# One row of norm weights spread by TensorE, and a hand-written order of half-block steps for the first tiles of a hybrid decoder trunk

## The chip, the cores and the metric

The kernel runs on one core of a Trainium2 chip. The metric is device time in microseconds, the median of several executions. Engines are named as in the profile: PE (TensorE, matrix products), ACT (ScalarE), DVE (VectorE), POOL (GpSimd) and SP (SyncE, which issues most of the DMA transfers).

## The reference

One layer of a decoder trunk over 1024 positions of 1024 features, with 16 learned meta tokens put in front (1040 rows). The part that matters here is its beginning:

```
def rmsnorm(x, gain):
    y = xf * lax.rsqrt(jnp.mean(xf * xf, axis=-1, keepdims=True) + EPS)
    return (y * gain)

h = concatenate([meta, x])
u = rmsnorm(h, mix_norm_pre)
proj = u @ w_in                 # 1024 x 4608
q, f_logit, i_in, g_out, v_pool, gate_a, gate_b = split(proj, cuts)
a = hgrn2(q, f_logit, i_in, g_out, ...)       # chunked linear recurrence
p = multiscale_pool(v_pool, ...)
z = sigmoid(gate_a) * (a @ w_branch_hgrn) + sigmoid(gate_b) * (p @ w_branch_pool)
h = h + rmsnorm(z @ w_out, mix_norm_post)
u = rmsnorm(h, ffn_norm_pre)
h = h + rmsnorm((gelu(dwconv(u @ w_gate)) * (u @ w_up)) @ w_down, ffn_norm_post)
```

The first columns that the kernel computes are those of `i_in` (512 columns), the "v" products.

## The kernel before, in words

Every fp32 product is made as three products of a shorter fp32 type: an operand is split into a `hi` part (a cast on ACT) and a `lo` part (a subtraction on DVE), and hi·hi, hi·lo and lo·hi are added up in a PSUM bank (`mm3`, lines 186 to 190).

The kernel begins with the rows. A tile is 128 rows. `vtiles` (L463) is the order in which the nine tiles (one of them the 16 meta rows) are taken. For each tile, `norm_steps` (L412) squares the row on ACT with a running sum, takes the root, makes the reciprocal on DVE, and multiplies row, reciprocal and gain in two halves (`scalar_tensor_tensor`, L420). The gain is a 128 x 1024 tile, `g1`, filled by one DMA that reads the 1024 weights once for every partition (`gain_bc`, L143). `feature_steps` (L426) then transposes the normalised row on PE in two groups of four, copies each group out of PSUM as `uhi` (L434, ACT) and subtracts for `ulo` (L436, DVE). The weights of the v products arrive in four blocks `raws` (`load_wi`, L457: two blocks of 128 rows by 512 columns each, side by side in one tile of 1024); `split_wi` (L511) casts one block whole (L516) and subtracts it whole (L517). The first three blocks' hi and lo parts lie in the buffers `whi` and `wlo`, three of each, which the later weights use again. `v_mm` (L520) makes the three products of one 128-row slice `k`.

Before the first row is ready, `warm` (L505) keeps PE busy with products of a constant matrix and the identity that go to an unused bank. Then the steps of tiles 0 and 1 follow in an order written out by hand, inside `tc.manual_schedule(engines={E.Activation, E.DVE, E.PE})`: on these engines the instructions run in the order in which they are written. On the others, SP among them, a planner orders them by its own timeline, and may put a later load ahead of an earlier store. Outside such blocks the planner orders all engines; that is so for the later stage of the recurrence heads.

After tiles 0 and 1 the loop over `vtiles[2:]` (L1081) makes each tile's 24 products, its features two tiles ahead, its norm four tiles ahead, sums of features that later products need (`gate_steps`, spread by `SUMS_AT`), and `v_out` (L530), which copies the bank out and stores it. In its last pass it makes `gl`, a `Loader` for two blocks of "G" weights: two loads into the raw buffers `wraw` (three of them), two casts and two subtractions into `whi` and `wlo` (`wsplit`, L149). Behind the loop come the first loads of the gate products (`gates.load_first`, L263 at the issue), the two G products, and then the gate products themselves, which a class `Strassen` makes by seven products P1 to P7 instead of eight. Units 0 to 3 begin with P1 and P2; `start_pair(2)` (L349) loads the pair of raw blocks of unit 0 (`load_unit`, L275 at the issue), of which POOL makes four sums (L282 to L285) for P5, P6, P7 and P3. `put_gate` stores results (L888).

Of the kernel before, what the change touches and what calls it, by code (L numbers as in the profile page):

```python
# [12 lines left out]
ALU = mybir.AluOpType  # L13
# [49 lines left out]
          "osg.2 sub2.2 sub32.1 sub8.1 wBA2 wBA6 wBA7 wBB2 wF0 wF2 wF3 wPP2 wPV0 wPV1 wQ0 wQ1 lq4.3 kdsub.1 qsmul.1 "  # L63
          "lk32.0 e1q.3 e1q.1 lq2.1 wQ2 sub2.3 rsl.0 lk32.3 lq64.1 qsmul.2").split()
TRUNC = False

CH_ALL = [(0, 348), (348, 346), (694, 346)]
CH_Q = [(0, CW), (CW, CW), (2 * CW, CW)]
# [3 lines left out]
def trunk_kernel(ctx: ExitStack, tc: tile.TileContext, x, meta_tokens, mix_norm_pre,  # L72
# [29 lines left out]
    def slot(n, dtype=F32, name="s"):  # L102
        return stage["fm", "p"].tile([P, n], dtype, tag="fm", name=nm(name), padded_shape=[P, LP])
# [17 lines left out]
    def small(shape, name, tag, bufs=4):  # L121
        return sm.tile(shape, F32, tag=tag, name=nm(name), bufs=bufs)

    def rr(a):
        return a.bitcast(F32)
# [7 lines left out]
    eps_t = const.tile([P, 1], F32, name="eps_t")  # L133
    dve.memset(eps_t, EPS)
    act.activation(small([P, 1], "std", "ns"), eps_t, AF.Sqrt)
    ident = const.tile([P, P], F32, name="ident")
    make_identity(nc, ident)
    onesm = const.tile([P, P], F32, name="onesm")
    pool_e.memset(onesm, 1.0 / P)
    onesr = const.tile([P, P], F32R, name="onesr")  # L140
    pool_e.tensor_copy(onesr, onesm)

    def gain_bc(src, name):  # L143
        t = slot(D, name=name)
        nc.sync.dma_start(t, src[0].partition_broadcast(P))
        return t
# [21 lines left out]
    class Loader:  # L168
# [10 lines left out]
        def next(self):  # L179
            self.at += 1  # L180
            return self.got[self.at - 1]
# [230 lines left out]
    def norm_steps(row, rows, gbc):  # L412
        ssq = small([P, 1], "ssq", "nq")
        un = slot(D, name="un")
        act.activation(un[:rows], row[:rows], AF.Square, accum_out=ssq[:rows])
        rstd = row_rstd(ssq, rows, "n")
        yield un
        for j in range(2):
            n = slice(j * 512, (j + 1) * 512)
            dve.scalar_tensor_tensor(un[:rows, n], row[:rows, n], rstd[:rows], gbc[:rows, n], ALU.mult, ALU.mult)  # L420
            yield un
# [29 lines left out]
    def load_row(t0, rows):  # L451
        row = slot(D, name="row")
        src = meta_tokens[:, :] if t0 == 0 else x[0, t0 - NM : t0 - NM + rows, :]
        nc.sync.dma_start(row[:rows], src)
        return row

    def load_wi(j):  # L457
        raw = slot(1024, name="wiraw")
        nc.sync.dma_start(raw.rearrange("p (k c) -> p k c", k=2), wblock(WIN, 2 * j, 2, CI, 512))
        return raw  # L460


    vtiles = [row_tiles[i] for i in (1, 5, 2, 6, 3, 7, 0, 4, 8)]  # L463
    rows_in = [load_row(*vtiles[0])]
    g1 = gain_bc(mix_norm_pre, "g1")
    raws = [load_wi(0)]
    rows_in.append(load_row(*vtiles[1]))
    raws += [load_wi(j) for j in range(1, 4)]
    rows_in += [load_row(*rt) for rt in vtiles[2:]]

# [34 lines left out]
    def warm(n):  # L505
        for _ in range(n):
            pe.matmul(junk_bank[:, :P], onesm, ident, start=True, stop=True)

    wi = []

    def split_wi(raw):  # L511
        if len(wi) < 3:
            hi, lo = (wst.tile([P, 1024], F32R, tag=t, name=nm(t)) for t in ("whi", "wlo"))
        else:
            hi, lo = slot(1024, F32R, "wihi"), slot(1024, F32R, "wilo")
        act.copy(hi, raw)  # L516
        dve.tensor_tensor(lo, raw, rr(hi), ALU.subtract)  # L517
        wi.append((hi, lo))

    def v_mm(ps, t0, k):  # L520
        hi, lo = wi[k // 2]
# [521 lines left out]

    vb = [bank("pv") for _ in range(2)]
    E = mybir.EngineType
    with tc.manual_schedule(engines={E.Activation, E.DVE, E.PE}):
        warm(14)
        n0, n1 = (norm_steps(rows_in[i], P, g1) for i in range(2))
        next(n0)
        next(n0)  # L1050
        un0 = next(n0)
        f0 = feature_steps(un0, P, uhi, ulo, vtiles[0][0])
        split_wi(raws[0])
        next(f0)
        next(f0)
        next(f0)
        next(n1)
        next(f0)
        next(n1)
        un1 = next(n1)  # L1060
        v_mm(vb[0], vtiles[0][0], 0)
        v_mm(vb[0], vtiles[0][0], 1)
        split_wi(raws[1])
        f1 = feature_steps(un1, P, uhi, ulo, vtiles[1][0])
        next(f1)
        next(f1)
        split_wi(raws[2])
        next(f1)
        next(f1)
        split_wi(raws[3])  # L1070
        for i, j in ((0, 1), (1, 0), (0, 2), (1, 1), (0, 3), (1, 2), (1, 3)):
            for k in (2 * j, 2 * j + 1):
                v_mm(vb[i], vtiles[i][0], k)
        v_norm(2)
        v_norm(3)
        for i in range(2):
            v_feat(2 + i)
            v_norm(4 + i)
        for i in range(2):
            v_out(vb[i], vtiles[i][0])  # L1080
        for i in range(2, len(vtiles)):  # L1081
            ps = bank("pv")
            for k in range(KD):
                v_mm(ps, vtiles[i][0], k)
            if i < 5:
                v_feat(i + 2)
            if i == 5:
                v_feat(7)
                v_feat(8)
            v_norm(i + 4)  # L1090
            if i == 3:
                params()
            if i == 5:
                for q in ("t2", "t1", "t3", "t4"):
                    two_halves(gq, q)
                sums = [gate_steps(d) for d in ds]
            if i == len(vtiles) - 1:
                gl = Loader([job("G", h)[:2] + (P,) for h in range(EARLY_G)])
            for j in SUMS_AT.get(i, ()):
                next(sums[j], None)  # L1100
            v_out(ps, vtiles[i][0])
        gates.load_first(0)
        gates.load_first(1)
        gates.ahead(2)
        for h in range(EARLY_G):
            src, n_k, xs, chunks, post = job("G", h)
            r = proj(None, 0, n_k, xs, chunks, ws=gl.next(), name="pg", by_bank=2 * h)
            if h == EARLY_G - 1:
                post(r)
            for j in SUMS_AT.get(9 + 2 * h, ()):  # L1110
                next(sums[j], None)
            if h < EARLY_G - 1:
                post(r)
            if h == 0:
                dve.tensor_tensor(vmeta[:NM], vm_hl[:NM], vm_low[:NM], ALU.add)
                gates.load_first(2)
                gates.ahead(4)
            for j in SUMS_AT.get(10 + 2 * h, ()):
                next(sums[j], None)

        close_pool("ps")
        open_pool("pf", 4, PSUM)
        gates.load_first(3)
        for e in range(0, EARLY, 2):
            p = gates.start_pair(e)
            for f in [f[i] for i in range(2) for f in p]:
                f()
                for j in SUMS_AT.get(13, ()) if e == 0 else ():
                    next(sums[j], None)
# [671 lines left out]
```

## Time and profile before

| what | value |
|---|---|
| median of 3 runs | 1330.11 us (1330.09 to 1330.13) |
| the profiled execution | 1330.1 us |
| its span, first to last instruction | 1328.4 us |
| PE busy | 1317.1 us, 99% |
| DVE, ACT, POOL busy | 970.7, 566.8, 440.4 us |

The profile shows one execution. In a row of the timeline the first number is the start in microseconds from the start of the span, the second the length; then come engine, line, operation, what is written and read, the shape, and how many such instructions are merged in the row. The bracket says how long the engine was idle before it and what ended the wait. In a row of windows there stand the length of the stretch and then the busy time of PE, PE's weight loads, DVE, ACT and POOL, the granted clock, the DMA share and GB/s.

### The profile page before, as it was taken

The numbers are of one execution on the slowest core, as the hardware profiler recorded it, in microseconds if no ns is written. First come the engines' busy times: TensorE is split into PE (matmuls) and PEld (weight loads), VectorE is DVE, ScalarE is ACT, GpSimd is POOL, SyncE is SP. The second block draws the span as 40 slices with busy tenths as digits, with TensorE's granted clock in tenths as the row PEclk, the third lists the DMA queues.
The fourth block names the chain that finished last, engine by engine and source line by source line (L and its number), as shares of the span: only waits on it lengthen the run. The fifth ranks groups of instructions, "written<-read, shape, count | busy, mean of one in ns | idle before, by whom it ended". The sixth has DMA issues, their size and how long they took to land.

```text
span 1328.4 us, 19923 instructions
## 1 busy us (share of the span) xinstructions
PE 1317.1 (99%) x7713; PEld 1177.6 (89%) x7713; DVE 970.7 (73%) x1229; ACT 566.8 (43%) x946; POOL 440.4 (33%) x327
## 2 busy tenths in 40 slices
PE   8999999999999999999999999999999999999997
PEld 7799899999999999987898888888888888888886
DVE  6765545389968777766578999888988885455758
ACT  5553333365556575235564222322222233444443
POOL 2015421226525720061025555545555652000000
PEclk9999999999999999999999999999999999999999
DMA  7134332411011157987686776676766799666644
GB/s 272 41 110 157 124 109 99 125 50 48 19 51 35 35 170 268 350 280 257 219 300 234 183 211 188 198 205 171 178 161 142 175 246 310 215 224 223 222 174 159
DMA packets 139665, 230.38 MB, mean 173 GB/s; under 512 B 9000, under 2 KB 77196, under 8 KB 139570
## 3 DMA queue, kind: packets, MB, share of 16 engines
q1 hardware_dynamic: 127506, 204.71, 45.3%
q0 software_dynamic: 12064, 24.38, 10.8%
q8 instruction: 61, 1.00, 0.3%
q14 instruction: 34, 0.28, 0.1%
HBM read 165.56 MB, written 86.53 MB: 190 GB/s over the span
## 4 chain that ended last, share of the span: by engine, by line
PE 95%; DVE 4%; DMA 0%; ACT 0%; issue 0%; SPq 0%; DVEq 0%
PE P L311 15%; PE P L312 15%; PE P L314 15%; PE pd L188 5%; PE pd L190 5%; PE pd L189 5%; PE pm L188 2%; PE pm L189 2%; PE pm L190 2%; PE sl L695 1%; PE ppv L208 1%; PE pbb L208 1%; PE ppv L212 1%; PE pbb L209 1%; PE ppv L209 1%; PE pbb L212 1%
## 5 line engine op out<-in xcount | busy, mean ns | idle before, releaser
L312 PE MATMUL P<-v,whi 128*128 128x512 f32 (+2 forms) x408 | 140.7, 353 | 0.0
L311 PE MATMUL P<-v,whi 128*128 128x512 f32 (+2 forms) x408 | 140.7, 352 | 0.0
L314 PE MATMUL P<-v,wlo 128*128 128x512 f32 (+2 forms) x424 | 135.1, 349 | 0.0
L1535 DVE TENSOR_TENSOR rot<-wraw,rot 128x1024 fp32r<-128x1024 f32 x31 | 38.0, 1225 | 72.3 <-ACT rot L1534 72.2
L282 POOL TENSOR_TENSOR swa<-wraw,wraw 128x512 f32<-128x512 f32 x28 | 42.3, 1510 | 133.0 <-DMA wraw<-in_ffn_w_gate_dram 69.3
L311 PEld LDWEIGHTS P<-v,whi 128*128 128x128 f32 x408 | 76.7, 188 | 10.4
L312 PEld LDWEIGHTS P<-v,whi 128*128 128x128 f32 x408 | 76.6, 188 | 10.2
L314 PEld LDWEIGHTS P<-v,wlo 128*128 128x128 f32 x424 | 74.0, 188 | 10.8
L256 ACT CAST whi<-wraw 128x512 fp32r<-128x512 f32 x78 | 46.1, 618 | 87.6 <-PE P L312 64.2
L190 PE MATMUL pd<-rot 128*128 128x512 f32 x272 | 82.1, 389 | 0.0
L189 PE MATMUL pd<-rot 128*128 128x512 f32 x272 | 82.1, 389 | 0.0
L188 PE MATMUL pd<-rot 128*128 128x512 f32 x272 | 81.1, 389 | 0.1
L1534 ACT CAST rot<-wraw 128x1024 fp32r<-128x1024 f32 x31 | 32.7, 1055 | 90.8 <-PE pd L190 89.4
L256 ACT CAST whi<-swa 128x512 fp32r<-128x512 f32 x56 | 33.4, 618 | 81.9 <-PE P L312 76.2
L1463 DVE SCALAR_TENSOR_TENSOR y<-g,par,y 128x1024 f32<-128x1024 f32 x44 | 64.5, 1467 | 0.8
L257 DVE TENSOR_TENSOR wlo<-swb,whi 128x512 fp32r<-128x512 f32 x56 | 59.9, 1075 | 6.9 <-ACT whi L256 6.9
L257 DVE TENSOR_TENSOR wlo<-wraw,whi 128x512 fp32r<-128x512 f32 x74 | 62.3, 864 | 2.7 <-ACT whi L256 2.7
L256 ACT CAST whi<-swb 128x512 fp32r<-128x512 f32 x56 | 33.4, 618 | 68.6 <-PE P L312 64.2
L188 PEld LDWEIGHTS pd<-rot 128*128 128x128 f32 x272 | 51.0, 188 | 11.1 <-DVE p L1471 0.5
L189 PEld LDWEIGHTS pd<-rot 128*128 128x128 f32 x272 | 51.1, 188 | 10.6
L190 PEld LDWEIGHTS pd<-rot 128*128 128x128 f32 x272 | 51.0, 188 | 10.6
L311 PE MATMUL P<-t4h,whi 128*128 128x258 f32 (+1 forms) x196 | 57.0, 307 | 0.0
(421 smaller groups left out, 4133.0 us busy)
## 6 DMA issues: line engine op xcount, KB each, us to landing
wraw<-in_w_in_dram SPq DMA_DIRECT2D x36, 512.0 KB, 4.0
yt<-ysum SPq DMA_DIRECT2D x33, 512.0 KB, 4.5
wraw<-in_ffn_w_gate_dram SPq DMA_DIRECT2D x26, 512.0 KB, 7.3
wraw<-in_ffn_w_up_dram SPq DMA_DIRECT2D x22, 512.0 KB, 6.1
wsum<-in_ffn_w_down_dram SPq DMA_DIRECT2D x22, 512.0 KB, 9.0
wraw<-in_w_out_dram SPq DMA_DIRECT2D x18, 512.0 KB, 5.5
ysum<-ys SPq DMA_DIRECT2D x11, 768.0 KB, 7.7
sa<-sscr SPq DMA_DIRECT2D x16, 513.0 KB, 6.8
```

What stands on the lines that cost most here:

```text
L188: pe.matmul(ps, ahi, bhi, start=first, stop=False)
L189: pe.matmul(ps, ahi, blo, start=False, stop=False)
L190: pe.matmul(ps, alo, bhi, start=False, stop=last)
L256: act.copy(hi, src)
L257: (pool_e if 4 <= i < 2 * self.early else dve).tensor_tensor(lo, src, rr(hi), ALU.subtract)
L282: pool_e.tensor_tensor(s1, a21, a22, ALU.add)
L311: pe.matmul(d, whi[:, k, :], xh[:, c : c + w], start=(k == 0 and onto is None), stop=False, **go)
L312: pe.matmul(d, whi[:, k, :], xl[:, c : c + w], start=False, stop=False, **go)
L314: pe.matmul(x[:, o : o + w], wlo[:, k, :], xh[:, c : c + w], start=False, stop=(k == 3), **go)
L1463: dve.scalar_tensor_tensor(a, g[:, j : j + SEQ], cvw[:, j, m : m + 1], a, ALU.mult, ALU.add)
L1534: act.copy(hi, src)
L1535: dve.tensor_tensor(lo, src, rr(hi), ALU.subtract)
```

## The change

The gain row is loaded once, as 4 KB in one partition, by a DMA that POOL issues ahead of making the identity. PE multiplies it with a row of ones into two PSUM banks, after 8 warming calls and ahead of 3 more (before: 14 in one go). Tile 0's own norm, `first_norm`, reads the gain from these banks. The broadcast load `g1` stays for the other tiles, and is issued behind row 1. Row 0 is loaded in two halves, and its square is taken in two halves. `split_wi` becomes a generator of four steps of half a block; the steps of norms (n), weight splits (s), features (f) and single products (m: hi·hi, x: hi·lo, y: lo·hi; first digit the tile, second the slice k) follow the list `START`. SP joins the engines of the written order, and the G weights' loader is made at `i == 6` and not in the last pass (i = 8).

```diff
+WARM = (8, 3)
+START = ("n0 n0 n0 s0 s0 f0 s0 s0 f0 f0 f0 m00 m01 x00 x01 y00 y01 n1 s1 n1 n1 s1 s1 s1 f1 f1 m02 y02 f1 x02 f1 "
+         "m03 y03 x03 m10 x10 y10 m11 x11 y11 s2 s2 s2 s2 m04 x04 y04 m05 y05 x12 y12 m13 x13 y13 x05 s3 s3 m12 s3 "
+         "s3 m06 x06 y06 m07 x07 y07 m14 x14 y14 m15 x15 y15 m16 x16 y16 m17 x17 y17")
...
     act.activation(small([P, 1], "std", "ns"), eps_t, AF.Sqrt)
+    grow = slot(D, name="grow")
+    nc.gpsimd.dma_start(grow[:1], mix_norm_pre[:, :])
     ident = const.tile([P, P], F32, name="ident")
     make_identity(nc, ident)
     onesm = const.tile([P, P], F32, name="onesm")
     pool_e.memset(onesm, 1.0 / P)
+    ones = slot(P, name="ones")
+    pool_e.memset(ones[:1], 1.0)
...
-    rows_in = [load_row(*vtiles[0])]
-    g1 = gain_bc(mix_norm_pre, "g1")
+    rows_in = [slot(D, name="row")]
+    halves = [slice(j * 512, (j + 1) * 512) for j in range(2)]
+    for n in halves:
+        nc.sync.dma_start(rows_in[0][:, n], x[0, vtiles[0][0] - NM : vtiles[0][0] - NM + P, n])
     raws = [load_wi(0)]
     rows_in.append(load_row(*vtiles[1]))
+    g1 = gain_bc(mix_norm_pre, "g1")
     raws += [load_wi(j) for j in range(1, 4)]
...
-    def split_wi(raw):
-        if len(wi) < 3:
+    def split_wi(j):
+        if j < 3:
...
-        act.copy(hi, raw)
-        dve.tensor_tensor(lo, raw, rr(hi), ALU.subtract)
         wi.append((hi, lo))
+        for n in halves:
+            act.copy(hi[:, n], raws[j][:, n])
+            yield
+        for n in halves:
+            dve.tensor_tensor(lo[:, n], raws[j][:, n], rr(hi[:, n]), ALU.subtract)
+            yield
+
+    def gain_row():
+        for n in halves:
+            ps = bank("gb")
+            pe.matmul(ps, ones[:1], grow[:1, n], start=True, stop=True)
+            yield ps
+
+    def first_norm(row):
+        ssq, un = [small([P, 1], "ssq", "nq") for _ in halves], slot(D, name="un")
+        for n, s_ in zip(halves, ssq):
+            act.activation(un[:, n], row[:, n], AF.Square, accum_out=s_)
+            if s_ is ssq[0]:
+                dve.tensor_scalar(s_, s_, 1.0 / D, EPS, ALU.mult, ALU.add)
+        std, rstd = small([P, 1], "std", "ns"), small([P, 1], "rstd", "nr")
+        act.activation(std, ssq[1], AF.Sqrt, bias=ssq[0], scale=1.0 / D)
+        dve.reciprocal(rstd, std)
+        yield un
+        for n, g in zip(halves, gain):
+            dve.scalar_tensor_tensor(un[:, n], row[:, n], rstd, g, ALU.mult, ALU.mult)
+            yield un
+
+    def v_part(i, k, part):
+        (uh, ul), (hi, lo) = (uhi, ulo), wi[k // 2]
+        t, c = slice(vtiles[i][0], vtiles[i][0] + P), slice((k % 2) * 512, (k % 2) * 512 + 512)
+        a, b = {"m": (uh, hi), "x": (uh, lo), "y": (ul, hi)}[part]
+        done[i] += 1
+        pe.matmul(vb[i], a[:, k, t], b[:, c], start=done[i] == 1, stop=done[i] == 3 * KD)
...
-    with tc.manual_schedule(engines={E.Activation, E.DVE, E.PE}):
-        warm(14)
-        n0, n1 = (norm_steps(rows_in[i], P, g1) for i in range(2))
...
+    with tc.manual_schedule(engines={E.Activation, E.DVE, E.PE, E.SP}):
+        warm(WARM[0])
+        gain = list(gain_row())
+        warm(WARM[1])
+        done = [0, 0]
+        steps = dict(n0=first_norm(rows_in[0]), n1=norm_steps(rows_in[1], P, g1))
+        for token in START.split():
+            kind, i = token[0], token[1:]
+            if kind in "mxy":
+                v_part(int(i[0]), int(i[1]), kind)
+                continue
+            if token not in steps:
+                if kind == "f":
+                    steps[token] = feature_steps(uns[int(i)], P, uhi, ulo, vtiles[int(i)][0])
+                else:
+                    steps[token] = split_wi(int(i))
+            un = next(steps[token], None)
+            if kind == "n":
+                uns[int(i)] = un
         v_norm(2)
         v_norm(3)
...
-            if i == len(vtiles) - 1:
+            if i == 6:
                 gl = Loader([job("G", h)[:2] + (P,) for h in range(EARLY_G)])
```

More of the change, by code (lines that the diff above doesn't have):

```diff
@@ L1045, in trunk_kernel @@
     E = mybir.EngineType
-    with tc.manual_schedule(engines={E.Activation, E.DVE, E.PE}):
-        warm(14)
-        n0, n1 = (norm_steps(rows_in[i], P, g1) for i in range(2))
[L1049 to L1073, printed above, removed]
+    with tc.manual_schedule(engines={E.Activation, E.DVE, E.PE, E.SP}):
[17 more added lines that the diff above has]
+                uns[int(i)] = un
         v_norm(2)
```

## The prediction

> **What bounds the kernel now.** I read the page first: how much of the span TensorE (PE) works, and which engine the chain that ended last runs through.
>
> ```profile
> span 1328.4 us, 19923 instructions
> PE 1317.1 (99%) x7713; PEld 1177.6 (89%) x7713; DVE 970.7 (73%) x1229; ACT 566.8 (43%) x946; POOL 440.4 (33%) x327
> PE 95%; DVE 4%; DMA 0%; ACT 0%; issue 0%; SPq 0%; DVEq 0%
> ```
>
> PE is busy for all but 11.3 us of 1328.4, and the chain is PE's own queue for 95%. So time is saved only where PE idles or does work that counts for nothing. The windows view says where that is.
>
> ```profile
> 0.00:24.00 24.00, 20.15 (x92) 16.35 (x93) 13.21 (x21) 12.88 (x22) 8.55 (x36) 1.00 0.94 329
> 24.00:110.00 86.00, 86.00 (x536) 77.74 (x535) 57.26 (x117) 46.66 (x106) 11.07 (x9) 1.00 0.29 94
> 300.00:480.00 180.00, 179.43 (x1408) 175.88 (x1407) 148.08 (x160) 104.03 (x170) 95.58 (x47) 1.00 0.13 38
> ```
>
> The second number after the length is PE's busy time. The first 24 us hold 3.85 us of idle PE; the next 86 us hold none, so whatever brings the first two tiles' products to their end earlier moves everything behind them by as much. Now the timeline of those 24 us (start, length, engine, line, operation).
>
> ```profile
> 0.80 0.20 POOL masks.py:197 MEMSET ident<- 128x128 f32 x1 [0.29 <-POOLq L1787]
> 1.53 5.91 PE L507 MATMUL pj<-ident,onesm 128*128 128x128 f32 x28 [1.53 <-POOL ident masks.py:199]
> 4.20 1.06 ACT L415 ACTIVATE un<-row 128x1024 f32<-128x1024 f32 x1 [1.91 <-DMA row<-in_x_dram]
> 5.17 0.19 ACT L415 ACTIVATION_READ_ACCUMULATOR un<-row 128x1 f32 x1
> 5.38 0.29 ACT L407 ACTIVATE std<-ssq,eps_t 128x1 f32<-128x1 f32 x1
> 5.71 0.16 DVE L409 RECIPROCAL rstd<-std 128x1 f32<-128x1 f32 x1 [4.78 <-ACT std L407]
> 6.56 1.43 DVE L420 SCALAR_TENSOR_TENSOR un<-row,rstd,g 128x512 f32<-128x512 f32 x2 [0.69 <-DMA g<-in_mix_norm_pre_dram]
> 7.47 1.23 PE L431 MATMUL pt<-ident,un 128*128 128x128 f32 x8
> 7.94 1.05 ACT L516 CAST whi<-wiraw 128x1024 fp32r<-128x1024 f32 x1 [2.26 <-DMA wiraw<-in_w_in_dram]
> 8.89 1.07 ACT L434 CAST uhi<-pt 128x512 fp32r<-128x512 f32 x2
> 9.02 1.23 DVE L517 TENSOR_TENSOR wlo<-wiraw,whi 128x1024 fp32r<-128x1024 f32 x1 [1.03 <-ACT whi L516]
> 9.53 0.49 PE L188 MATMUL pv<-whi,uhi 128*128 128x512 f32 x1 [0.82 <-ACT uhi L434]
> 10.18 0.68 DVE L436 TENSOR_TENSOR ulo<-pt,uhi 128x512 fp32r<-128x512 f32 x1
> 12.92 1.23 PE L431 MATMUL pt<-ident,un 128*128 128x128 f32 x8 [0.82 <-DVE un L420]
> 14.63 0.50 PE L189 MATMUL pv<-wlo,uhi 128*128 128x512 f32 x1 [0.24 <-DVE wlo L517]
> 24.04 1.91 PE L431 MATMUL pt<-ident,un 128*128 128x128 f32 x16
> ```
>
> The row lands at 4.2, the reciprocal is done at 5.87, and the first half of the normalised row then waits for the broadcast gain until 6.56. PE fills that time with 28 instructions that count for nothing (14 calls, so a plain f32 product is two instructions). Tile 0's transposes start at 7.47. Up to 14.63 PE waits by turns for copies, casts and subtractions; from there 41 products run to 24.04, 0.23 us each, without a hole. Transposes to end: 16.57 us.
>
> **The clock.** The 28 instructions take 0.211 us each; the last four and later ones of the same size do not:
>
> ```profile
> 6.82 0.62 PE L507 MATMUL pj<-ident,onesm 128*128 128x128 f32 x4
> 439.14 1.79 PE sb L763 x16
> 603.36 0.57 POOL L1244 DMA_DIRECT2D wlos<-wlo  x1 [0.30 <-POOL wlo L1243]
> ```
>
> Sixteen in 1.79 us are 0.112 each. So PE runs at half rate until about 6.7, some 5.2 us after its first instruction, although the windows view gives a granted clock of 1.00 for the stretch. The third row is what one DMA issue costs POOL, 0.57 us.
>
> **Part by part: the start.** The new gain path: POOL issues the 4 KB load of the gain row before it makes the identity. That issue takes 0 (if POOL makes the identity first) to 0.57 us; I take 0.57, as it is written first, so PE's warming starts at 2.10 and not at 1.53. The load itself has about 4.7 us (0.8 to 5.5) before PE asks for it. Eight warming calls are 16 x 0.213 = 3.41, to 5.51. Then the gain is spread by two f32 products of 512 columns: four instructions, each four times a 128-column one, 0.85 us at half rate and 0.45 at full rate (no such row in the trace; the bounds are these two, from the L507 and L763 rows). With the clock changing at 6.7 as now: the first ends at 6.36, the second at 6.96, the others at 7.4 and 7.85. Three warming calls, 6 x 0.11, end at 8.5. PE takes its queue in order, so tile 0's transposes start at 8.5, a full microsecond later than now, although the row in halves makes the reciprocal no later (about 5.45: the second half's square is half of 1.06, then 0.19, 0.29, 0.16 as in the rows). The gain's DMA wait of 0.69 goes; PE's own spreading is what is late in its place. Bounds of this start: 7.8 where the clock changes as the gain products begin and the issue is short, 9.6 where it changes only as they end.
>
> What follows, with the rows' lengths (STT 0.72, cast and copy of 512 0.55, DVE 0.62 to 0.68): un halves at 7.9 and 8.75; transposes 8.5 and 8.95; copies of uhi at 9.15 to 10.25; the casts of the first weight block were done by 6.7, ahead of them, where now the copy stands behind a 1.05 us cast; DVE then makes the two wlo halves by 10.05 and the ulo halves by 11.3. ACT squares row 1 from 10.2, std ends 11.7; DVE: reciprocal 11.9, un halves 12.7 and 13.4, wlo of block 1 at 14.0 and 14.65, ulo 15.25. PE: six products between 9.75 and 11.5, transposes 12.8, two products, transposes 13.7, four products, and at 15.05 it is free for tile 1 with 12 products done and nothing late ahead of it. 36 products x 0.23 = 8.3: end at 23.3. From the transposes that is 14.8 us against 16.57: the half-block steps and the new order are worth 1.75, and the start gives 1.0 of it back. Net 24.04 - 23.3 = **0.7 us gained**; with the bounds of the start 7.8 and 9.6, from 1.4 gained to 0.4 lost. The later place of the gain's broadcast load (behind row 1) is hidden: the first four and a half transfers of 512 KB at the 329 GB/s of the 0:24 row are 7.2 us, so by about 9 it is in, and the first use is at 11.95.
>
> **Part by part: SP in written order.** SyncE (SP) is now in the hand-written order, so loads no longer slip ahead of stores.
>
> ```profile
> 19.02 1.38 SPq L151 DMA_DIRECT2D wraw<-in_w_in_dram  x2
> 62.82 1.06 ACT L154 CAST whi<-wraw 128x1024 fp32r<-128x1024 f32 x1 [0.77 <-PE pv L190]
> 65.90 0.38 SPq L263 DMA_DIRECT2D wraw<-in_w_in_dram  x1
> 97.61 0.37 SPq L275 DMA_DIRECT2D wraw<-in_w_in_dram  x1
> 102.33 0.34 SPq L888 DMA_DIRECT2D sscr<-sg  x1
> 101.25 1.29 POOL L282 TENSOR_TENSOR swa<-wraw,wraw 128x512 f32<-128x512 f32 x1
> 105.09 0.62 ACT L256 CAST whi<-swa 128x512 fp32r<-128x512 f32 x1 [2.79 <-POOL swa L283]
> 105.61 0.58 ACT L346 COPY p<-P 128x514 f32<-128x514 f32 x1
> 112.19 0.29 PE L311 MATMUL P<-t2h,whi 128*128 128x258 f32 x1
> wraw<-in_w_in_dram SPq DMA_DIRECT2D x36, 512.0 KB, 4.0
> ```
>
> The G weights' loads (L151), issued at 19.02 now, will stand behind the store of vtile 5 and be issued near 55. Their casts (L154) wait in any case for tile 8's products to free the buffers, at 62.82, so PE loses nothing. But moved to i == 6 the casts stand on ACT ahead of two v copies and of sums, and hold ACT and DVE for some 8 us; the products of tiles 7 and 8 need neither, and the sums are used only from 112 on. I cost that at 0.
>
> The one place where the order bites is unit 0's pair of weight loads (L275). Its second half is issued at 97.61 now; in written order both stand behind the store of 102.33, so they go out at 102.7 and 103.1 and land near 107.5 (4.0 us median). POOL's sums, 1.29 each, start then and not at 101.25: the third, which P6 needs, ends at 111.4; the cast to 112.0; the copy behind it on ACT (the 105.61 row), which frees the bank pair that P6 writes, at 112.6. P6 starts at 112.19 now. The 7 us that lie between the 105.09 cast and 112.19 are thus used up, and about **0.4 us are lost** (bounds: 0 if POOL makes P6's sum second, 1.5 if the load and store share the DMA engines and land a microsecond later).
>
> **The sum.** The profiled execution took 1330.1 us for a span of 1328.4 (1.7 us lie around it), the median of the runs is 1330.11, so no scaling. 1330.1 - 0.7 + 0.4 = **1329.8**. Its own range, from the bounds: 1328.7 to 1332.0. A difference of 0.2%, 2.66 us, is about what a measurement of this kernel can tell from no change.
>
> **Rivals.** (a) Clock released early. PE reaches full rate as the eight warming calls end, at 5.5: the gain products take 4 x 0.45, transposes start at 7.9, the end is 22.7; 1330.1 - 1.3 + 0.4 = 1329.2. Against it: now the change comes 5.2 us after PE's start. Beside it: the Trainium skill, "TensorE: Matmul & The Clock Gate", Part 1, says that a busy window of about 3.4 us releases the clock and that these windows run freely; the earliest case of that rule is this rival, and the 5.2 us of the trace also fit it, with a first window only half filled. 0.15.
>
> (b) Slower: the spreading keeps PE cold. The place is PE's queue between 5.5 and 8.9: the gain products use one row of the array, and if they do not count as activity, or the gain row lands late and PE idles, all 22 warming instructions and the four long ones run at half rate: 2.1 + 22 x 0.213 + 4 x 0.85 = 10.2 for the transposes, which then cost 8 x 0.10 more, and the first six products up to 6 x 0.2. End 25.0 + 0.8 + 1.2 = 27.0, 3.0 later than now, and with the 0.4: 1333.5. It decides from a transpose start of about 9.8 with the clock still low. For it: no row shows a one-row product. Against: the warming fills the time before it. 0.12.
>
> (c) Faster by more than 0.2%: transposes at 6.6 or before (un is possible from 6.2), which needs short gain products and a clock released at once, or less waiting in 300 to 480, where DVE is 148 of 180 us busy and the order isn't written by hand: a new start can reorder it. PE's idle there is only 0.57 us by the view, so little is to be had. 24.04 - (6.4 + 14.8) = 2.8: 1327.3. 0.14.
>
> (d) The same reordering with the other sign, or loads that come later than costed: a few microseconds of PE idle in that stretch, say 3: 1332.9. 0.06.
>
> **How the numbers follow.** Forecast 0.53 and (a) 0.15 lie within 0.2%: together 0.68, less 0.01 of tail. Faster 0.14; slower 0.12 + 0.06 and that tail, 0.19. The range reaches from 1327.5, leaving out most of (c), to 1332.9, leaving out half or more of (b).
>
> **What would show it.** Right: the gain products as four rows of 0.45 to 0.85 us between 5.5 and 8; transposes of tile 0 at about 8.5; steady products from about 15, transposes of tiles 2 and 3 at 23.3; L275 behind L888; POOL's first sum near 107.5 and P6 with its start just held. Wrong: transposes at 10 with products of 0.4 us pitch (b), transposes before 7 (c), or PE idle that is not now there between 300 and 480 (c, d).

## The result, and the profile after

The changed kernel took 1334.66 us (median of 8 runs, 1332.91 to 1337.83) against 1330.12 us before (8 runs, 1330.07 to 1331.08): a ratio of 1.0033, 95% interval 1.0024 to 1.0042. It is slower by 0.33%, and outside the predicted range. The eight times lie in two groups, 1332.91 to 1333.30 (four runs) and 1336.02 to 1336.34 (three), with the profiled run, 1337.83, above both. The median is thus only the middle of the gap between the groups (between 1333.30 and 1336.02): no run took it. The later group lies well above the range, the early one just above its end of 1332.9. Why there are two groups 3.1 us apart is part of what has to be explained.

Page of the changed kernel: span, busy time by engine, the chain that ended last.

```profile
span 1336.1 us, 19929 instructions
PE 1321.0 (99%) x7711; PEld 1179.1 (88%) x7711; DVE 972.6 (73%) x1234; ACT 567.5 (42%) x952; POOL 441.7 (33%) x329
PE 93%; DVE 4%; DMA 2%; ACT 1%; issue 0%; POOL 0%; SPq 0%; DVEq 0%; ACTq 0%; POOLq 0%
```

PE is busy 3.9 us longer than before with two instructions fewer, so its instructions became longer, and its idle time grew by 3.8 us (15.1 against 11.3). The windows view says where (length, PE, PE's weight loads, DVE, ACT, POOL, granted clock, DMA share, GB/s).

```profile
0.00:24.00 24.00, 19.84 (x76) 15.07 (x77) 12.36 (x24) 13.84 (x28) 8.33 (x38) 1.00 0.80 289
110.00:300.00 190.00, 187.57 (x1225) 175.50 (x1224) 103.42 (x132) 76.54 (x125) 61.09 (x42) 1.00 0.36 114
300.00:480.00 180.00, 179.45 (x1416) 176.24 (x1415) 149.10 (x160) 104.08 (x172) 97.07 (x47) 1.00 0.13 38
```

In the first 24 us PE executes 76 instructions in place of 92, in about the same busy time. Between 110 and 300 it idles 2.43 us. Between 300 and 480 it idles 0.55 us, as before (0.57). Now the timeline of the start.

```profile
1.35 0.68 POOL L141 DMA_DIRECT2D grow<-in_mix_norm_pre_dram  x1 [0.84 <-POOLq L1820]
2.02 0.24 POOL masks.py:197 MEMSET ident<- 128x128 f32 x1
2.89 3.78 PE L518 MATMUL pj<-ident,onesm 128*128 128x128 f32 x16 [2.89 <-POOL ident masks.py:199]
4.87 0.63 ACT L544 ACTIVATE un<-row 128x512 f32<-128x512 f32 x1 [0.61 <-DMA row<-in_x_dram]
5.95 0.16 DVE L549 RECIPROCAL rstd<-std 128x1 f32<-128x1 f32 x1 [1.51 <-ACT std L548]
6.61 3.78 PE L538 MATMUL gb<-grow,ones 1*128 1x512 f32 x4
8.71 0.75 DVE L552 SCALAR_TENSOR_TENSOR un<-row,rstd,gb 128x512 f32<-128x512 f32 x1 [2.60 <-PE gb L538]
10.31 1.65 PE L518 MATMUL pj<-ident,onesm 128*128 128x128 f32 x6
11.75 1.92 PE L439 MATMUL pt<-ident,un 128*128 128x128 f32 x8
13.49 1.10 PE L560 MATMUL pv<-whi,uhi 128*128 128x512 f32 x2
16.80 0.63 PE L439 MATMUL pt<-ident,un 128*128 128x128 f32 x4 [1.27 <-ACT whi L529]
27.27 1.91 PE L439 MATMUL pt<-ident,un 128*128 128x128 f32 x16
```

POOL's issue of the gain row starts only at 1.35 and takes 0.68, and the identity stands behind it, so PE's first instruction is at 2.89, not at 1.53. The four gain instructions run from 6.61 to 10.31, 0.93 us each. The six warming instructions behind them, 1.44 us from start to start of what follows, and the eight transposes of tile 0 at 11.75, 1.92 us against 1.23 before, are at half rate as well. No engine makes PE wait between 2.89 and the products: it is slow, not idle. Tiles 2 and 3 start their transposes at 27.27 (before: 24.04), 3.23 us late.

Later on, at unit 0 of the gate products and at the passage from the gates to the heads:

```profile
105.54 0.34 SPq L930 DMA_DIRECT2D sscr<-sg  x1
105.98 1.55 SPq L283 DMA_DIRECT2D wraw<-in_w_in_dram  x3
112.14 1.29 POOL L290 TENSOR_TENSOR swa<-wraw,wraw 128x512 f32<-128x512 f32 x1 [7.61 <-DMA wraw<-in_w_in_dram]
114.64 1.28 POOL L291 TENSOR_TENSOR swa<-swa,wraw 128x512 f32<-128x512 f32 x1
115.96 0.62 ACT L264 CAST whi<-swa 128x512 fp32r<-128x512 f32 x1 [10.44 <-POOL swa L291]
116.48 0.58 ACT L354 COPY p<-P 128x514 f32<-128x514 f32 x1
117.12 0.39 PE L319 MATMUL P<-t2h,whi 128*128 128x258 f32 x1 [1.54 <-ACT p L354]
252.21 0.40 PE L216 MATMUL pf<-uhi,whi 128*128 128x348 f32 x1 [0.87 <-DVE sg L926]
565.87 0.42 PE L216 MATMUL pba<-ah,whi 128*128 128x342 f32 x1 [1.14 <-ACT whi L172]
```

The chain can be read downwards: store, the loads of unit 0 behind it, POOL's sum when they land, the third sum, ACT's cast of it, ACT's copy of the bank behind the cast, and P6 at 117.12. Before, P6 started at 112.19 without a wait. With the 3.23 us already lost it would start at 115.42; it starts 1.70 later, and 2.1 with the short waits inside it. At the passage (before: 245.88) 1.0 us more is lost, at the projection at 565.87 (before: 558.16) another 1.4. So the profiled run lost 3.2 + 2.1 + 1.0 + 1.4 = 7.7 us, and that is what the spans differ by (1336.1 against 1328.4). In the last 1.4 PE waits for a cast on ACT; the profile puts that wait down to a store (`kept9h`) that landed 7.7 us behind its issue, against 6.5 before. Without them this run would lie beside the later group, so by the times they come in some runs only.

### The profile page after: what moved, and what is told of

It reads as the page before. It is cut to its first block, busy times and chain, and to the rows that moved or that the text cites. A ratio compares the mean times of both kernels' runs of the same rounds, so it can differ in the third digit from the quotient of the medians.

```text
span 1336.1 us, 19929 instructions
## 1 busy us (share of the span) xinstructions
PE 1321.0 (99%) x7711; PEld 1179.1 (88%) x7711; DVE 972.6 (73%) x1234; ACT 567.5 (42%) x952; POOL 441.7 (33%) x329
## 4 chain that ended last, share of the span: by engine, by line
PE 93%; DVE 4%; DMA 2%; ACT 1%; issue 0%; POOL 0%; SPq 0%; DVEq 0%; ACTq 0%; POOLq 0%
PE P L319 14%; PE P L322 14%; PE P L320 14%; PE pd L196 5%; PE pd L197 5%; PE pd L198 5%; PE pm L196 2%; PE pm L197 2%; PE pm L198 2%; PE sl L737 1%; PE ppv L216 1%; PE pbb L216 1%; PE ppv L220 1%; PE pbb L217 1%; PE pbb L220 1%; PE ppv L217 1%
## 5 line engine op out<-in xcount | busy, mean ns | idle before, releaser
L320 PEld LDWEIGHTS P<-v,whi 128*128 128x128 f32 x408 | 76.6, 188 | 10.2
L319 PE MATMUL P<-t2h,whi 128*128 128x258 f32 (+1 forms) x196 | 56.9, 307 | 1.5 <-ACT p L354 1.5
```

The source lines that it names most:

```text
L319: pe.matmul(d, whi[:, k, :], xh[:, c : c + w], start=(k == 0 and onto is None), stop=False, **go)
L320: pe.matmul(d, whi[:, k, :], xl[:, c : c + w], start=False, stop=False, **go)
```

## The experiments

Each kernel ran 8 to 12 times beside the kernel before, which took 1330.13 to 1330.24 on these chips. Short names: "the spread" is the gain row's load by POOL, the products with ones and the split warming; "SP written" is SP in the written order with the G loader at `i == 6`. My first theory had two parts: the spread costs the start (late warming, then a clock not released), and SP written costs unit 0's weights.

**The changed kernel without SP written.**

```diff
-    with tc.manual_schedule(engines={E.Activation, E.DVE, E.PE, E.SP}):
+    with tc.manual_schedule(engines={E.Activation, E.DVE, E.PE}):
-            if i == 6:
+            if i == len(vtiles) - 1:
```

> The changed kernel with SP left to the planner and the G loader back in the last pass; spreading and half-block steps stay. Theory: no wait at P6 and none at the passage to the heads; what is left is the start, which differs between executions by the moment of the clock's release: some near 1330.1, some near 1333.3. Rival (these waits come from the late start and not from SP's order): still about 2.9 us more, 1333 to 1336.

1331.33 us (six runs from 1330.13 to 1331.33, five from 1333.21 to 1333.35), ratio 1.0009, 1.0001 to 1.0018. Timeline and windows of its profiled run, one of the early group (1330.13):

```profile
2.88 3.67 PE L518 MATMUL pj<-ident,onesm 128*128 128x128 f32 x16 [2.88 <-POOL ident masks.py:199]
6.47 1.98 PE L538 MATMUL gb<-grow,ones 1*128 1x512 f32 x4
9.16 1.37 PE L439 MATMUL pt<-ident,un 128*128 128x128 f32 x8
9.00:10.00 1.00, 1.00 (x10) 1.00 (x10) 1.00 (x3) 0.21 (x1) 0.97 (x3) 0.86 1.02 291
10.00:11.00 1.00, 1.00 (x4) 0.63 (x3) 1.00 (x2) 0.81 (x2) 0.00 (x0) 0.50 0.97 356
110.00:300.00 190.00, 190.00 (x1249) 178.52 (x1248) 106.29 (x135) 78.36 (x129) 57.80 (x39) 1.00 0.33 106
```

PE starts as late as in the changed kernel, but here the gain instructions take 1.91 us together and not 3.70, and the transposes start at 9.16. That is the difference between the two groups. The end of the two tiles is 0.09 us later than before. The idle time between 110 and 300 is gone.

The two rows of 1 us show something more. PE is busy all the time, and still the granted clock falls: 0.86 on average from 9 to 10, then 0.50; finer stretches put the fall at 9.7 and the return at 13.1. Of the 3.4 us ahead of the fall, 1.9 were the one-row gain products. So the clock was released by the warming, and lost again without any idle time. The loss costs little here, since PE has to wait for ACT behind it anyway (0.35 us at 13.66; with the clock high, in the run with 128 rows below, 1.26 at the same place).

**The kernel before with SP written, and nothing else.**

```diff
-    with tc.manual_schedule(engines={E.Activation, E.DVE, E.PE}):
+    with tc.manual_schedule(engines={E.Activation, E.DVE, E.PE, E.SP}):
-            if i == len(vtiles) - 1:
+            if i == 6:
```

> The kernel before with SP in the written order and the G loader at i == 6, and nothing else. Theory: a start as before (transposes of tiles 2 and 3 at 24.04), P6 of unit 0 held for 1.5 to 2 us behind the late load of its weights, 1.0 us at the passage to the heads: 1333.0, executions alike. Rival (the wait at the heads comes from the late start): 1332.0. Rival (SP's order costs nothing by itself): 1330.1.

1334.22 us (1332.91 to 1336.76), ratio 1.0028, 1.0019 to 1.0037. Its profiled run took 1333.05. Windows and timeline:

```profile
110.00:300.00 190.00, 187.85 (x1226) 175.78 (x1225) 105.57 (x135) 77.78 (x128) 60.79 (x41) 1.00 0.34 109
113.58 0.39 PE L311 MATMUL P<-t2h,whi 128*128 128x258 f32 x1 [1.26 <-ACT p L346]
248.68 0.40 PE L208 MATMUL pf<-uhi,whi 128*128 128x348 f32 x1 [0.88 <-DVE sg L884]
```

The two losses appear without the new start: P6 1.8 us late by its end, the heads 2.8 in all. The expected 1333.0 came in four of eleven runs; the executions are not alike, and what the runs above 1333.3 add, 1.2 us in the median, was not traced.

**The changed kernel with unit 0's loads ahead of the last store.** In the loop that makes and stores P1 and P2 of the early units, the loads go out before the last store.

```diff
-            for f in [f[i] for i in range(2) for f in p]:
+            for n_, f in enumerate([f[i] for i in range(2) for f in p]):
                 f()
+                if e == 0 and n_ == 2:
+                    gates.load_unit(gates.run[0])
```

> The changed kernel with the pair of loads for unit 0 written one product earlier, between the stores of the first two gate results. Theory: they land about 3 us earlier, P6 of unit 0 does not wait (offset against before stays level there, 1.9 us less), while the step of 1.0 us at the passage to the heads stays or goes with the choice of banks: time 1.9 to 2.9 us under the changed kernel in executions with the same start, 1330.1 to 1331.1 and 1333.2 to 1334.2. Rival (P6's wait has another cause, the casts or the banks): no step less than 1.5 us at P6, times as the changed kernel's.

1333.21 us: four runs from 1330.03 to 1330.20, one at 1331.91, five from 1333.21 to 1333.74, one at 1336.80; ratio 1.0016, 1.0006 to 1.0025. The start of its profiled run (1333.27) is that of the changed kernel, transposes at 11.75. But:

```profile
110.00:300.00 190.00, 190.00 (x1250) 178.52 (x1248) 106.87 (x135) 77.76 (x128) 60.84 (x42) 1.00 0.35 110
109.58 1.29 POOL L290 TENSOR_TENSOR swa<-wraw,wraw 128x512 f32<-128x512 f32 x1 [5.05 <-DMA wraw<-in_w_in_dram]
```

POOL's first sum starts 2.6 us earlier, P6 starts on time, and the 1.0 us at the heads go with it, although nothing was changed there. So one late pair of loads costs about 3 us, at two places (2.8 in the run before this one, 3.1 in the changed kernel). The two groups remain, at 1330.1 and 1333.3: they are made at the start.

**A gain product that fills all rows of the array.** The product has the same length, but is made of a constant 128 x 512 tile and `onesm`; tile 0's gain is left out.

```diff
+    full = slot(512, name="full")
+    dve.memset(full, 1.0)
...
-            pe.matmul(ps, ones[:1], grow[:1, n], start=True, stop=True)
+            pe.matmul(ps, onesm, full, start=True, stop=True)
```

> The changed kernel, but the two gain products read a full 128-row constant instead of one row (tile 0 is left without its gain). Same number, width and place of PE instructions. Theory (a one-row product holds PE but does not count as the activity that releases its clock): now the clock is released during or before the second gain product in every execution, transposes at 8.7 to 10, and the slow group of executions near 1336 goes: all near 1333, median 1333.0. Rival (only the moment at which the clock is looked at decides): still two groups 3 us apart, 1333 and 1336, median near 1334.7.

1332.75 us, ten runs in one group from 1332.23 to 1333.81 and one at 1338.30; ratio 1.0023, 1.0014 to 1.0032.

```profile
6.45 1.98 PE L540 MATMUL gb<-full,onesm 128*128 128x512 f32 x4
8.94 1.04 PE L441 MATMUL pt<-ident,un 128*128 128x128 f32 x8
0.00:24.00 24.00, 19.63 (x94) 15.97 (x95) 14.29 (x27) 13.85 (x28) 8.76 (x38) 1.00 0.80 290
```

With one row in use, the later group held four of eight runs in the changed kernel, and five and six of eleven without SP written and with the early loads; with 128 rows, at most one of eleven. The profiled run has the clock released ahead of the gain products, like the one without SP written (gain products from 6.45 here, from 6.47 there); but with 128 rows the granted clock stays at 1.00 to the end of the start. The start ends 0.4 us earlier than before, and the loss that is left is SP's.

**Warming split 6 and 5.** The kernel with the early unit 0 loads, the same work on PE, but less of it ahead of the one-row products.

```diff
-WARM = (8, 3)
+WARM = (6, 5)
```

> The kernel with unit 0's loads ahead of the store, and the eleven warming calls split 6 and 5 in place of 8 and 3; nothing else. The work on PE is the same, and without a hole, from 2.89 on: 12 warming instructions of 0.23 to 5.7, the four gain instructions, 10 warming instructions. Theory (one-row products don't count towards releasing the clock): what stands ahead of the gain products is now 2.8 us of counted work in place of 3.7, too little to release it in any execution, so all are as the later group was with 8 and 3: gain products 0.9 each, transposes of tile 0 at 11.8, 1333.2 to 1333.8, and none near 1330.1. Rival 1 (one-row products count, and the two groups come from something else at the start): the unbroken work is the same, so the two groups stay, 1330.1 and 1333.3, in shares like 5 and 6 of 11. Rival 2 (what matters is only how long PE has worked, by any product): one group near 1330.1 to 1330.5, transposes at 9.2.

1333.37 us, eleven runs from 1333.21 to 1335.30 and one at 1329.69; ratio 1.0022, 1.0014 to 1.0031.

```profile
2.88 2.93 PE L518 MATMUL pj<-ident,onesm 128*128 128x128 f32 x12 [2.88 <-POOL ident masks.py:199]
5.74 3.78 PE L538 MATMUL gb<-grow,ones 1*128 1x512 f32 x4
11.74 1.91 PE L439 MATMUL pt<-ident,un 128*128 128x128 f32 x8
```

Theory: none early; it was one of twelve. The two rivals wanted half or all of them early. In the profiled run PE works without a hole from 2.88 on and is still at half rate past 11.74; by their times, so are eleven of the twelve. What it works on from 5.74 to 9.45 has one row. The share of early runs thus goes by the work ahead of the one-row products, not by all unbroken work.

**The gain row loaded by SP, behind the row's halves.**

```diff
-    nc.gpsimd.dma_start(grow[:1], mix_norm_pre[:, :])
...
+    nc.sync.dma_start(grow[:1], mix_norm_pre[:, :])
     raws = [load_wi(0)]
```

> The changed kernel with the 4 KB gain row loaded by SP behind row 0's halves, so that POOL makes the identity first. Theory (1.36 us of the late start are POOL's DMA issue): PE's warming starts at 1.5 and not at 2.9, the whole start moves 1.4 us earlier in executions with the same clock, but still two groups: 1332 and 1335. Rival (POOL's issue is hidden): no change against the changed kernel.

1334.71 us: three runs from 1331.62 to 1332.08, five from 1334.66 to 1335.08, one at 1336.76; ratio 1.0027, 1.0018 to 1.0037. In its profiled run (1331.65) the gain products start at 5.37 and the transposes at 8.05, and the two tiles end 1.3 us earlier than before; the SP losses are unchanged. Here the granted clock stays at 1.00 behind the one-row products: they do not make it fall in every run. POOL's issue thus costs the start 1.2 to 1.4 us, and has nothing to do with the two groups.

**The row in halves, alone.** The kernel before, with row 0 loaded by two transfers.

```diff
-    rows_in = [load_row(*vtiles[0])]
+    rows_in = [slot(D, name="row")]
+    for j in range(2):
+        nc.sync.dma_start(rows_in[0][:, j * 512 : (j + 1) * 512], x[...])
```

> The kernel before with row 0's load cut into two halves and nothing else. Theory (two loads of 2 KB pieces at the head of the queue slow what stands behind them): the broadcast gain lands at 8.4 to 8.9 and not at 6.5, the transposes start 1.5 to 2.3 us later, 1331.6 to 1332.5. Rival (the late gain of e1 and e3 came from something else): within 0.3 us of the kernel before.

1333.05 us (1332.17 to 1335.72), ratio 1.0023, 1.0014 to 1.0032.

```profile
8.78 1.41 DVE L420 SCALAR_TENSOR_TENSOR un<-row,rstd,g 128x512 f32<-128x512 f32 x2 [2.47 <-DMA g<-in_mix_norm_pre_dram]
9.67 1.23 PE L431 MATMUL pt<-ident,un 128*128 128x128 f32 x8 [1.94 <-DVE un L420]
11.54 0.80 PE L188 MATMUL pv<-whi,uhi 128*128 128x512 f32 x1 [0.64 <-ACT uhi L434]
```

The broadcast gain, next in SP's queue, lands at 8.78 and not at 6.56. PE stands idle for 1.94 us ahead of the transposes and 0.64 us ahead of the products, and from there its products are at half rate (0.80 for 0.49): finer windows show the granted clock at 0.50 from 10.9, as the transposes end, to 17.7. The two tiles end at 26.73, 2.7 us late. The gain landed as expected, but the median is 0.5 us above the expected range, which counted only the later transposes.

**The new order without the spread,** with SP written (first) and planned (second). Gain from `g1`, whose load stands behind the row's halves.

```diff
-    grow = slot(D, name="grow")
-    nc.gpsimd.dma_start(grow[:1], mix_norm_pre[:, :])
...
+    g1 = gain_bc(mix_norm_pre, "g1")
     raws = [load_wi(0)]
     rows_in.append(load_row(*vtiles[1]))
-    g1 = gain_bc(mix_norm_pre, "g1")
...
-        warm(WARM[0])
-        gain = list(gain_row())
-        warm(WARM[1])
+        warm(14)
+        gain = [g1[:, n] for n in halves]
...
```

> The changed kernel without the spreading: no load by POOL, 14 warming calls in one go, tile 0 multiplies with the broadcast gain, whose load stands behind row 0 again; the half-block steps and SP in written order stay. Theory (the spreading on a cold PE makes the start late, SP's written order costs 1.9 us at P6 and 1.0 us at the passage to the heads): tile 0's transposes at 7.5, end of the two tiles near 22.3, 1330.1 - 1.7 + 2.9 = 1331.3, and executions that agree within 0.5 us. Rival (the half-block order is itself what makes the start late): the end of the two tiles stays above 24.5 and the time above 1333.

> The half-block steps, the row in halves and the new order of steps alone: no spreading, SP left to the planner. Theory: transposes at 7.5, 14.8 us from there to the end of the two tiles instead of 16.57, nothing lost later: 1330.1 - 1.7 = 1328.4, all executions alike, faster than both kernels. Rival (the order of steps is at fault): 1330 or more.

1334.40 us (1333.42 to 1336.04; ratio 1.0029, 1.0018 to 1.0040) and 1332.01 us (1330.76 to 1333.63; 1.0010, 1.0001 to 1.0018). Both expectations failed, by 3 and 4 us, and this is how the halves were found. Timeline of the second:

```profile
8.92 1.41 DVE L548 SCALAR_TENSOR_TENSOR un<-row,rstd,g 128x512 f32<-128x512 f32 x2 [3.28 <-DMA g<-in_mix_norm_pre_dram]
9.73 1.97 PE L435 MATMUL pt<-ident,un 128*128 128x128 f32 x8 [3.04 <-DVE un L548]
```

The 28 warming instructions had taken 5.16 us, so the clock was released in them; after 3.04 idle us the eight transposes run at half rate (1.97). Finer windows show the granted clock at 0.50 from 8.7 to 15.5, after 2.0 us without work.

**The half-block order alone.** Row 0 whole, its norm as before, gain by DMA as before, SP planned: only `START` and the half-block weight steps stay. The rest of the edit is that of the second kernel above.

```diff
-    for n in halves:
-        nc.sync.dma_start(rows_in[0][:, n], x[...])
+    rows_in = [load_row(*vtiles[0])]
...
-        steps = dict(n0=first_norm(rows_in[0]), ...)
+        steps = dict(n0=norm_steps(rows_in[0], P, g1), ...)
```

> As e3_order_alone, but row 0 in one load and one square (its norm as in the kernel before): only the half-block steps of the weights and the new order are left. Theory (the row in halves slows the first loads, so that the gain's load landed at 8.9 instead of 6.5 and PE, idle for 3 us, lost its clock): gain at 6.5, transposes at 7.5, clock kept, end of the two tiles at 22.3, 1328.4. Rival (the loads' lateness is chance of the chip or comes from the order of steps): as e3, 1331 to 1332.

1329.33 us (1328.93 to 1330.68), ratio 0.9994, 0.9986 to 1.0003. It is the fastest version found, 0.8 us below the kernel before, but the interval still holds no difference. It was expected at 1328.4: the gain and the transposes came as expected and the clock stayed, but the two tiles end at 23.29 and not at 22.3.

```profile
7.64 1.23 PE L435 MATMUL pt<-ident,un 128*128 128x128 f32 x8 [0.80 <-DVE un L424]
8.20 1.14 ACT L523 CAST whi<-wiraw 128x512 fp32r<-128x512 f32 x2 [2.30 <-DMA wiraw<-in_w_in_dram]
9.88 0.73 PE L554 MATMUL pv<-whi,uhi 128*128 128x512 f32 x2 [1.01 <-ACT uhi L438]
```

From the transposes to the end it takes 15.65 us where the kernel before took 16.57, so the order is worth 0.9 here. ACT takes the first weights' two casts at 8.20, when they land, ahead of the copy that PE waits for; I take it that the order would be worth more with weights that come sooner, but no run tests that.

**Both mends at once, full rows and early unit 0 loads.** The gain row is loaded by SP into a zero-filled 128-row tile, and the ones fill 128 rows, so that the products still spread the gain. The second kernel has two warming calls fewer.

```diff
+    dve.memset(grow, 0.0)
+    nc.sync.dma_start(grow[:1], mix_norm_pre[:, :])
...
-            pe.matmul(ps, ones[:1], grow[:1, n], start=True, stop=True)
+            pe.matmul(ps, ones, grow[:, n], start=True, stop=True)
```

> The changed kernel with three causes taken away together: the gain row is loaded by SP into the first row of a tile of zeros (POOL makes the identity first), the spreading multiplies all 128 rows (result unchanged), and unit 0's loads are written ahead of the second gate store. Theory (each of the three was shown by itself): start as the early executions of e9_gain_row_by_sp (end of the two tiles 1.3 us earlier than in the kernel before), no steps later, one group of executions: 1328.8, faster than both kernels. Rival (the causes overlap, or the tile of zeros holds the loads): 1330 or more, or two groups.

> As e10_full_rows_early_unit with one warming call behind the gain products instead of three. Theory (PE's own queue holds the transposes back): transposes about 0.4 us earlier, at 7.6, then the normalised row decides: 1328.4 to 1328.8. Rival (ACT's wait for the first weights decides already): as e10.

1331.68 us (1329.11 to 1333.28; ratio 1.0005, 0.9997 to 1.0014) and 1330.33 us (1329.49 to 1333.23; 1.0004, 0.9994 to 1.0013). The first missed its 1328.8:

```profile
1.12 0.91 DVE L475 MEMSET grow<- 128x1024 f32 x1 [0.19 <-issue]
7.01 3.75 PE L539 MATMUL gb<-grow,ones 128*128 128x512 f32 x4 [1.56 <-DMA grow<-in_mix_norm_pre_dram]
11.39 1.04 PE L437 MATMUL pt<-ident,un 128*128 128x128 f32 x8
```

The zero fill ends at 2.03, the load cannot start before it and lands late, and the clock is low through the gain products, this time with all rows in use; I put that down to the idle 1.56 us ahead of them. But it is released as they end, so the transposes are fast (1.04 for eight), where behind four one-row products of the same length in the changed kernel they took 1.92. All but one of the 128 rows hold zeros here, so it is the number of rows that counts and not the numbers in them. The second kernel missed its 1328.4 to 1328.8 in the same way: its gain products wait 0.86 us and run at half rate, and its transposes start at 10.29. The mend brought the start's loss back in another form.

## Why the prediction was wrong, point by point

*POOL's issue, 0 to 0.57, warming from 2.10.* Wrong in its start. The issue took 0.68, near the 0.57 of its row, but began at 1.35: warming from 2.89. I had bounded the issue's length and not its start.

*Price of the gain instructions, 0.85 and 0.45.* Near: 0.93 each at half rate, 1.91 / 4 = 0.48 at full rate. The difference has a reason that I could have read: my 0.213 per warming instruction is a mean that holds the fast last ones too. At half rate sixteen of them took 3.72 us, 0.23 each.

*Clock at 6.7 as before, transposes at 8.5 (7.8 to 9.6).* This step failed, and it makes the later group. I took the release as a fixed time, when it follows what PE has done before, and I let one-row products count as such work. In the traced run of the early group the release came ahead of 6.47, the transposes at 9.16, within the bounds, and then the clock was lost again from 9.7 to 13.1, which no line of the prediction has. In the later group the release came only past 13, and the transposes at 11.75. Rival (b) named the cause, one-row products that do not count, and the place. It had a chance of 0.12, because "the warming fills the time before it"; but eight calls from 2.89 release the clock in about half the runs only. The experiments with 128 rows and with 6 and 5 calls, and the clock that falls behind one-row products without an idle moment, bear (b) out. Its price, 3.0 us later for the end of the tiles against 3.2 measured, is right by luck: the transposes come 1.5 us later than its 10.2, and from there to the end it takes 15.5 us and not 16.8.

*Row in halves, costed at nothing, with a reciprocal at 5.45.* Wrong: the second half landed at 4.87 where the whole row had landed at 4.20, and the reciprocal ended at 6.11, later than before's 5.87. Alone it delays the gain behind it by 2.2 us. In the changed kernel the spread covers that, since tile 0 no longer needs the broadcast.

*Transposes to the end, 14.8.* Right where the clock stayed high: 23.63 - 8.94 = 14.7 with 128 rows, and 22.74 - 8.05 = 14.7 with the gain row loaded by SP. Without SP written it is 24.13 - 9.16 = 15.0, with the clock low for 3.4 us of it. The changed kernel's 15.5 contain the slow transposes and first products; the order alone gives 15.65, with transposes that come earlier and weights that do not.

*G loads, 0.* Right: with unit 0's loads mended, PE is busy without a hole from 24 to 300.

*Unit 0's loads, 0.4 (0 to 1.5).* The chain was right step by step, and the term mis-sized: P6 alone came 1.7 late, 2.1 with its short waits. This step failed in every run, and with the passage to the heads it puts even the early group, near 1333.0, just above the end of the range. The sum assumed 4.0 us from issue to landing, the median of all such loads; POOL's first sum started 6.2 us behind the first issue of the pair (105.98 to 112.14), with the last store just ahead of it and another load of the same line behind it. The runs with SP alone and with the loads ahead of the store show 5.9 and 6.5.

*The passage to the heads.* Not in the prediction: 1.0 us. PE there waits for a bank that DVE still reads. The run with the earlier loads loses nothing there, so it follows from them; that another bank was chosen because of the late pair is how I read it, and no run isolates it.

*Rivals (c) and (d), the stretch from 300 to 480.* Neither: 0.55 us idle against 0.57.

The range ended at 1332.9, which left out half or more of rival (b) by intent, and never added (b) to a late unit 0. The two add: the runs without one or the other show 0.1 or 3.2 at the start and 2.8 from SP, and 1330.1 + 2.8 + 0.1 = 1333.0 and 1330.1 + 2.8 + 3.2 = 1336.1 are the two groups of the changed kernel. With rival (b) and the upper bound of the SP term, the prediction's own numbers give 1330.1 + 3.0 + 1.5 = 1334.6; that this meets the median of 1334.66 is chance, since the median lies between the groups.

What stays open: the wait at the projection, 1.14 us at 565.87 here and 1.51 at the same place with the row in halves alone, and what lengthens the other runs above their groups. Open too is how much of a stretch must be full work for the clock to be released or kept: the fall behind one-row products came in one traced run and not in another.

## What to carry to other kernels

Warming is a budget of counted work, not of time: whatever is put between it and the first real products must itself be work that counts, and must not wait. Putting a queue in written order is priced at the one transfer that used to slip ahead, with the landing time of that place and not the median, and followed to the engine's later stages. Cutting a first load in two is not free for the loads queued behind it.

## What the runs showed of the hardware

One-row products as activity: with 3.7 us of full warming ahead of 3.7 us of one-row work the clock was released early in about half the runs (late were four of eight, five and six of eleven, and six of nine), with 2.8 us ahead in 1 of 12; with 128 rows in the same work in at least 10 of 11. In one run the clock was withdrawn from 9.7 to 13.1 while PE never idled. The granted clock of the windows view reads 1.00 from the start of each trace, also while PE is at half rate; there the rate is read from the lengths of like instructions, 0.93 against 0.48. A later loss it does show, as 0.50.

The Trainium skill, "TensorE: Matmul & The Clock Gate", Part 1, says that windows of about 3.4 us run freely, that one busy window releases the clock, and that the transition varies from run to run. Two groups of runs of the same program agree with free-running windows, and so do the low stretches of the granted clock: 3.4 us without SP written, and 6.8 us, twice that, with halves alone and in the new order without the spread. If a window had to be busy throughout, an estimate from the 3.4 us would let 2.8 us of warming never do, and 3.7 us in about a tenth of the runs; the shares were 1 of 12 and about half, so less than a full window must be enough. Its rule for losing the clock, a gap of over about 3.4 us, asks for more than was seen: the clock fell after gaps of 1.75 and 1.94 us (the new order without the spread and with SP written; halves alone), and once without a gap. In this the measurement decides.

POOL's DMA issue, written ahead of the identity, began 1.35 us after the span's start; in the kernel before, the identity's first memset starts at 0.80. Two transfers of 256 KB in place of one of 512 KB slowed the stretch around them; windows of 4 to 5 and 5 to 6 us, the kernel before and the one with halves alone (length, DVE, granted clock, DMA share, GB/s):

```profile
4.00:5.00 1.00, 0.00 (x0) 1.00 0.92 213
5.00:6.00 1.00, 0.16 (x1) 1.00 0.93 252
```

```profile
4.00:5.00 1.00, 0.00 (x0) 1.00 0.87 139
5.00:6.00 1.00, 0.00 (x0) 1.00 0.84 199
```

The transfer engines are nearly as busy (0.87 and 0.84 against 0.92 and 0.93) and move a third less and a fifth less. Why is not shown.
